# RWKV-7 hybrid layer: other places for the pooling branch in the dense order, and earlier turns for the recurrence

## The chip, the cores and the metric

The kernel runs on one core of a Trainium2 chip. The metric is the device time of one execution in microseconds (us); the time before is the median of 3 runs. TensorE (PE) multiplies matrices, with PEld as its weight loads; VectorE (DVE), ScalarE (ACT) and GpSimd (POOL) work elementwise; SyncE (SP) issues most DMAs. Each engine works off its own queue in order.

## The reference

One step of a hybrid decoder layer for 1024 prompt tokens and 8 x 8 sample tokens, 1088 columns in all, with the same weights. Cut to what matters here:

```
h = rms_norm(x, norm_mix) * (1 + sc) + sh
P = h @ w_in                          # RWKV columns | pooling columns | gate columns
# branch A: RWKV-7, 8 heads of 64
for t:                                # wkv7_scan
    sa = S @ (-kk_t)
    S = S * w_t + sa x (kk_t * a_t) + v_t x k_t
    y_t = S @ r_t
o_r = (group_norm(y) * ln_w + ln_b + bonus) * g
# branch B: pooling over 2, 4, 8 and 16 tokens, four groups of 128 channels
pooled = (cs[t] - cs[t - win]) / count - pp
o_p = einsum("btgc,gcd->btgd", pooled, pool_w) * pool_scale
# merge, then the mixer
merged = sigmoid(gate_A) * (o_r @ w_br_rwkv) + sigmoid(gate_B) * (o_p @ w_br_pool)
x = x + gt * (merged @ w_out)
x = x + gt2 * (relu(h2 @ w_ff1)**2 @ w_ff2);  y = rms_norm(x)
```

## The kernel before

Features lie on the 128 partitions, tokens along the columns. A dense product is done in three parts, high weights by high and low activations and low weights by high activations (whi and wlo against hx), over three chunks of columns (364, 362, 362) into three PSUM tiles called mm. A block of 128 columns of weights is a job: its weights are loaded, split (whi by ScalarE L227, wlo by VectorE L228) and multiplied, and each chunk is then copied out by its own consumer (L573 for projections, L606 and L684 for others).

Phase 1, to about 720 us, holds the input projection and all of the recurrence. Its dense jobs are a list: X are the RWKV columns, Q(g) the columns of pooling group g, G the gates, and at the end op_load (which loads the pooled rows) and eight branch jobs op_job, whose consumer is L1405. Beside the jobs stand four foreground programs written as coroutines, which issue small work in between: the chain of the recurrence over 16 chunks of 64 tokens; the pools, which run, per group, three pooling matmuls of 364, 362 and 298 + 64 columns (px by plw), each copied out by ScalarE (L683) and VectorE (L684); the heads, which for each of four head pairs f go through front (group norms and decay: products wt by sw into two banks, tanh by ScalarE L725), burst (the scan of the decay on VectorE, L751 to L767), unit (products of two sets of 8 chunks), inverse, level and affine; and or_rows.

Affine has two rounds u, each first(u) (64x64 products into two banks, copied by ScalarE L1005 to L1007) and second(u): 16 products ab by at into two banks, four chunks to a bank, read by VectorE L1025 and L1026. Beside affine stand front(f + 1) and the group norm, joined by a helper called both.

The small work has four PSUM banks under two tags, w (2) and wc (2); the mm tiles have four. When a bank is freed decides whether the next step can start. A class Pace makes the order of TensorE's work when the program is built: it counts a virtual time t with estimated lengths, and lets the foreground go on when its step's time has come and a bank is free by its own estimate (free()); otherwise it fills in dense work. A step yields the time after which it goes on, and that time is also taken as the time at which its bank is free again (between 1500 and 3600 ns). The order on the other engines, and which bank a tile gets, are made by the framework's scheduler from there.

Of the kernel before, what the change touches and what calls it, by code (L numbers as in the profile page):

```python
# [83 lines left out]
class Pace:  # L84
# [3 lines left out]
    def __init__(self):  # L88
        self.t = 0.0
        self.work = []  # L90
        self.dense = False
        self.taken, self.banks, self.gap, self.held = None, {"w": [0.0, 0.0], "wc": [0.0, 0.0]}, 1500, False

    def take(self):

# [6 lines left out]

    def free(self):
        return min(self.banks[x][0] for x in (["w"] if self.held else ["w", "wc"])) <= self.t

    def give(self, r):
        for tag in self.taken:
# [24 lines left out]
    def run(self, back, fore=(), until=lambda: False):  # L132
        self.back = back
        live = {i: 0.0 for i in range(len(fore))}
        busy = True
        while (live or busy) and not until():
            for i in sorted(live):
                r = live[i]
                if self.taken is not None and i and not self.free() and (i == 2 and not isinstance(r, Off) and not hasattr(r, "own") or i == 1 and not callable(r) and self.t < r + 1200):
                    continue  # L140
                if r() if callable(r) else r <= self.t:
                    if self.taken is not None:
                        self.taken, self.gap = [], 1500
                    try:
                        r = next(fore[i])
                        if self.taken:
                            self.give(min(max(self.gap if callable(r) else r, 1500), 3600))
                        live[i] = r if callable(r) else type(r)(self.t + r)
                    except StopIteration:
                        del live[i]  # L150
                    break
            else:
                r = "idle"
                if busy:
                    try:
                        r = next(back)
                    except StopIteration:
                        busy = False
                self.dense = r != "idle"
                if r == "idle" and live:  # L160
                    self.t += 100
# [9 lines left out]
class K:  # L171
# [526 lines left out]
    def front(self, f, got=None):  # L698
# [18 lines left out]
        for i, (c0, n) in enumerate(((0, 512), (512, 512), (1024, 64))):  # L717
# [3 lines left out]
            yield 800  # L721
        for c0, n in FP:
            ps = self.ps("w")
# [95 lines left out]
    def unit(self, f, d, u):  # L819
# [13 lines left out]
        Q = dict(ab=tl("ab", [2, 128]), ak=tl("ak", [64], 1), uv=tl("uv", [2, 64]), ra=d["qs"][u]["ra"])  # L833
# [8 lines left out]
        for a in range(0, C, 4):  # L842
            m = min(4, C - a)
            us = slice(a, a + m)
            cu = slice(c0 + a, c0 + a + m)
            pss = [self.ps("w") for _ in HB]
            for i in range(m):
                for hs, ps in zip(HB, pss):
                    self.mm(ps[:, i * 128:(i + 1) * 128], bk[hs, c0 + a + i, :, :].rearrange("p s j -> p (s j)"),
                            ra[hs, a + i, :, :].rearrange("p s j -> p (s j)"), start=True, stop=True)  # L850
            for h, (hs, ps) in enumerate(zip(HB, pss)):
                os = HB[1 - h]
                pv = ps[:, :m * 128].rearrange("p (c s j) -> p c s j", s=2, j=64)
                pr, pa = (pv[:, :, h, :], pv[:, :, 1 - h, :]) if not prompt else (pv[:, :, 0, :], pv[:, :, 1, :])
                nc.vector.tensor_tensor(ab[:, us, h, 0:64], pr, incl.unsqueeze(1).to_broadcast([P, m, 64]), op=ALU.mult)
                nc.vector.tensor_tensor(ak[hs, us, :], pa[hs], strict[hs].unsqueeze(1).to_broadcast([64, m, 64]), op=ALU.mult)
                for b in range(2):
                    rq = slice(os.start + 32 * b, os.start + 32 * b + 32)
                    src = pa[rq, :, 32 * b:32 * b + 32]
                    if prompt:  # L860
                        nc.scalar.activation(ad[rq, cu, :], src, AF.Copy)
                        if b == 0:
                            nc.scalar.activation(ao[rq, cu, :], pa[rq, :, 32:64], AF.Copy)
                    else:
                        nc.vector.tensor_tensor(ad[rq, 16, :], src[:, 0, :], strict[rq, 32 * b:32 * b + 32], op=ALU.mult)
            yield 3500
        bh = bk[:, cs, :, :].rearrange("p c s j -> p c (s j)")
        if prompt:
            nc.vector.tensor_tensor(bh, bh, end[:, cs].unsqueeze(2).to_broadcast([P, C, 128]), op=ALU.mult)
# [122 lines left out]
    def affine(self, f, d):  # L992


        nc, z = self.nc, d["z"]

        def first(u):
            Q = d["qs"][u]
            uv, w = Q["uv"], Q["at"]
            pw, pu = self.ps("w"), self.ps("w")  # L1000
            for i in range(8):
                for h, os in enumerate((HB[1], HB[0])):
                    self.mm(pw[os, i * 64:(i + 1) * 64], z[os, 8 * u + i, :], w[os, i, :], start=True, stop=True)
                    self.mm(pu[os, i * 64:(i + 1) * 64], z[os, 8 * u + i, :], uv[os, i, h, :], start=True, stop=True)
            nc.scalar.activation(w, cut(pw), AF.Copy)  # L1005
            nc.scalar.activation(uv[HB[1], :, 0, :], cut(pu[HB[1], :]), AF.Copy)
            nc.scalar.activation(uv[HB[0], :, 1, :], cut(pu[HB[0], :]), AF.Copy)  # L1007

        def second(u):
            Q = d["qs"][u]  # L1010
            ab, ra, w = Q["ab"], Q["ra"], Q["at"]
            dg = cut(self.hv())
            for hs in HB:
                nc.gpsimd.tensor_tensor(dg[hs], self.kc("ident")[hs, hs].unsqueeze(1).to_broadcast([64, 8, 64]),
                                        d["end"][hs, 8 * u:8 * u + 8].unsqueeze(2).to_broadcast([64, 8, 64]), op=ALU.mult)
            pss = [self.ps("w") for _ in range(2)]
            for i in range(8):
                for h, hs in enumerate(HB):
                    os = HB[1 - h]
                    self.mm(pss[i // 4][hs, i % 4 * 128:(i % 4 + 1) * 128], w[os, i, :], ab[os, i, h, :], start=True, stop=True,  # L1020
                            tile_position=(os.start, hs.start))
            for a, ps in enumerate(pss):
                pv = ps.rearrange("p (c s j) -> p c s j", s=2, j=64)
                us = slice(4 * a, 4 * a + 4)
                nc.vector.tensor_tensor(ra[:, us, 1, :], pv[:, :, 1, :], dg[:, us, :], op=ALU.add)  # L1025
                nc.vector.tensor_tensor(ra[:, us, 0, :], ra[:, us, 0, :], pv[:, :, 0, :], op=ALU.add)  # L1026

        for u in range(2):
            first(u)
            yield 2500  # L1030
            second(u)
            self.done.add(("s", f, u))
            yield 3600

    def chain(self, f, d):

# [100 lines left out]
    def post(self, f):  # L1137
# [28 lines left out]
        def norm(c0, n):  # L1166

            for a, m in FP:
                if c0 <= a < c0 + n:
# [82 lines left out]
    def both(self, a, fill):  # L1252

        pace = self.pace
        live = [[a, pace.t], [fill, pace.t]]
        now = lambda: [x for x in live if (x[1]() if callable(x[1]) else x[1] <= pace.t) and (isinstance(x[1], Off) or pace.free())]
        some = lambda: bool(now())
        some.own = True
        while live:
            ready = now()  # L1260
            if not ready:
                yield some
                continue
            x = ready[0]
            try:
                r = next(x[0])
                x[1] = r if callable(r) else type(r)(pace.t + r)
                if pace.taken:
                    pace.gap = 1500 if callable(r) else r
                    yield some  # L1270
            except StopIteration:
                live.remove(x)
# [57 lines left out]
    def phase1(self, ctx):  # L1330
# [10 lines left out]
        X = self.rwkv_cols  # L1341
        J12, J4 = X(12, act=tanh_lo), X(4, tags=("mm", "w", "w"))

        G = [self.gate(18 + i, self.d_th[i]) for i in range(16)]
        Q = [self.pool_cols(g) for g in range(4)]
        jobs = [X(0), X(8), X(5), X(1), X(9), X(6), X(2), X(10), X(13, act=sigm), X(7), X(3), X(11)]
        for g in range(4):
            jobs += [Q[g], G[2 * g], G[2 * g + 1]] if g < 3 else [G[6], Q[3], G[7]]
        jobs += G[8:]
        order = [(j, h, q) for h in range(2) for q in range(4) for j in (J4, J12)] + [(j, h) for j in jobs for h in range(2)]  # L1350
        order += [(self.op_load, 0)] + [(self.op_job(m), 0) for m in range(8)]
        with ExitStack() as cs:
# [689 lines left out]
def cut(t):  # L2042
    return t.rearrange("p (c j) -> p c j", j=64)
# [12 lines left out]
NC = 17  # L2056
FH = [(0, 512), (512, 576)]
FP = [(0, 512), (512, 288), (800, 288)]
LS = (2000, 2000, 2000, 1500)
FW = 5500  # L2060
WB = (2, 2)
# [77 lines left out]
```

## Time and profile before

| | before |
|---|---|
| time, median of 3 | 1620.5 us (1619.76 to 1621.67) |
| profiled execution: its own time | 1620.03 us |
| profiled execution: span | 1618.2 us |
| TensorE busy | 1583.4 us, 98% |
| weight loads (PEld) | 1481.7 us, 92% |
| VectorE / ScalarE / GpSimd busy | 1022.9 / 736.1 / 356.5 us |
| mean granted TensorE clock | 0.996 |

The span is that of the profiled execution, from its first instruction to its last; its own time is a little longer. In rows of a timeline the first number is the start and the second the length in us, then engine, line, operation, out<-in, partitions x elements and count; what stands in brackets is the idle time of the engine before it and what ended it. A wait row has the sum, the number and the longest.

### The profile page before, as it was taken

How to read it: one execution, taken by the hardware profiler on the slowest of the kernel's cores; microseconds unless marked ns; L12 is line 12 of the kernel's file. 1: busy time of each engine (PE TensorE's matmuls, PEld its weight loads, DVE VectorE, ACT ScalarE, POOL GpSimd, SP SyncE). 2: the span in 40 equal slices, each digit the busy share in tenths (PEclk: the TensorE clock that was granted, in tenths of full speed). 3: DMA queues.
4: the chain of work that ended last, by engine and by line, in shares of the span. 5: the costliest groups of instructions: out<-in, count | busy, mean ns of one | idle time of the engine just before them, and what ended most of it. 6: DMA issues, size and time to landing. Idle time of an engine off the chain costs nothing.

```text
span 1618.2 us, 35474 instructions
## 1 busy us (share of the span) xinstructions
PE 1583.4 (98%) x14331; PEld 1481.7 (92%) x14331; DVE 1022.9 (63%) x1747; ACT 736.1 (45%) x1491; POOL 356.5 (22%) x464
## 2 busy tenths in 40 slices
PE   5999999999999999999999999999999999999997
PEld 3999888998898889979989999999999999999997
DVE  5685674846565636244635597777555777787866
ACT  5543343344335433432325475554455765553323
POOL 3301200120001000101513322333233243521231
PEclk9999999999999999999999999999999999999998
DMA  9334423423423242746875466667666865674313
GB/s 336 110 119 145 140 65 107 132 83 115 126 101 115 76 138 89 294 144 216 332 261 175 144 199 215 206 223 256 234 209 234 312 201 186 197 265 154 100 40 111
DMA packets 123333, 279.43 MB, mean 173 GB/s; under 512 B 16769, under 2 KB 31105, under 8 KB 123169
## 3 DMA queue, kind: packets, MB, share of 16 engines
q1 hardware_dynamic: 107808, 228.52, 41.7%
q0 software_dynamic: 9312, 32.41, 6.0%
q10 hardware_dynamic: 6048, 16.23, 2.8%
q8 instruction: 113, 1.85, 0.5%
q14 instruction: 52, 0.42, 0.1%
HBM read 198.15 MB, written 78.95 MB: 171 GB/s over the span
## 4 chain that ended last, share of the span: by engine, by line
PE 61%; DVE 2%; issue 2%; ACT 2%; DMA 1%; POOL 1%; DVEq 0%; SPq 0%; ACTq 0%; POOLq 0%
PE pr L204 30%; PE mm L204 22%; PE w L204 4%; PE wc L204 4%; DVE hx L1815 0%; DMA wr<-in_w_ff 0%; POOL wlo L228 0%; PE wc L211 0%; DVE hx L1984 0%; DMA wraw<-in_w_ff 0%; PE w L211 0%; POOL wr L1788 0%; DMA d_th<-px 0%; ACT hx L1738 0%; ACT mr L1738 0%
## 5 line engine op out<-in xcount | busy, mean ns | idle before, releaser
L204 PE MATMUL mm<-hx,whi 128*128 128x362 f32 (+1 forms) x1920 | 504.8, 344 | 0.8 <-ACT px L573 0.8
L204 PEld LDWEIGHTS mm<-hx,whi 128*128 128x128 f32 x1920 | 330.1, 189 | 34.0 <-issue 16.1
L204 PE MATMUL pr<-mr,whi 128*128 128x272 f32 x1792 | 336.4, 287 | 0.5 <-DVE hx L1815 0.2
L204 PE MATMUL mm<-hx,wlo 128*128 128x362 f32 (+1 forms) x960 | 314.1, 327 | 0.0
L204 PEld LDWEIGHTS pr<-mr,whi 128*128 128x128 f32 x1792 | 280.8, 188 | 2.7 <-issue 2.7
L204 PE MATMUL pr<-mr,wlo 128*128 128x272 f32 x896 | 257.9, 288 | 0.0
L227 ACT ACTIVATE whi<-wraw 128x512 fp32r<-128x512 f32 x186 | 116.8, 629 | 222.1 <-PE mm L204 86.3
L228 DVE TENSOR_TENSOR wlo<-wraw,whi 128x512 fp32r<-128x512 f32 x145 | 107.5, 742 | 132.2 <-ACT whi L227 130.3
L204 PEld LDWEIGHTS mm<-hx,wlo 128*128 128x128 f32 x960 | 181.3, 189 | 0.0
L204 PE MATMUL pr<-hx,whi 128*128 128x272 f32 x896 | 168.8, 287 | 1.4 <-DVE rs L2010 0.8
L204 PEld LDWEIGHTS pr<-mr,wlo 128*128 128x128 f32 x896 | 168.6, 188 | 0.2 <-DVE wlo L228 0.2
L204 PE MATMUL mm<-mr,whi 128*128 128x272 f32 (+4 forms) x736 | 152.3, 301 | 0.0
L204 PEld LDWEIGHTS pr<-hx,whi 128*128 128x128 f32 x896 | 140.3, 188 | 2.7 <-ACT whi L227 1.0
L227 ACT ACTIVATE whi<-wr 128x512 fp32r<-128x512 f32 x138 | 86.3, 627 | 113.8 <-PE pr L204 76.3
L204 PE MATMUL pr<-hx,wlo 128*128 128x272 f32 x448 | 128.9, 288 | 0.0
L204 PEld LDWEIGHTS mm<-mr,whi 128*128 128x128 f32 x736 | 119.2, 188 | 3.0 <-issue 2.5
L204 PE MATMUL mm<-mr,wlo 128*128 128x272 f32 (+4 forms) x368 | 110.1, 299 | 0.0
L228 POOL TENSOR_TENSOR wlo<-wraw,whi 128x512 fp32r<-128x512 f32 x41 | 54.8, 1337 | 217.8 <-ACT whi L227 217.6
L228 DVE TENSOR_TENSOR wlo<-wr,whi 128x512 fp32r<-128x512 f32 x103 | 76.7, 747 | 18.3 <-ACT whi L227 18.2
L204 PE MATMUL pr<-t,whi 128*128 128x272 f32 x448 | 84.6, 287 | 0.0
L204 PEld LDWEIGHTS pr<-hx,wlo 128*128 128x128 f32 x448 | 84.3, 188 | 0.0
L204 PEld LDWEIGHTS pr<-t,whi 128*128 128x128 f32 x448 | 70.2, 188 | 0.8 <-issue 0.8
(466 smaller groups left out, 2711.0 us busy)
## 6 DMA issues: line engine op xcount, KB each, us to landing
wr<-in_w_ff SPq DMA_DIRECT2D x137, 256.0 KB, 3.5
hid<-d_ch POOLq DMA_DIRECT2D x72, 272.0 KB, 3.9
wraw<-in_w_ff SPq DMA_DIRECT2D x71, 256.0 KB, 3.2
wraw<-in_w_in SPq DMA_DIRECT2D x68, 256.0 KB, 3.1
d_ch<-hx SPq DMA_DIRECT2D x52, 272.0 KB, 3.8
hid<-in_w_ada_mlp SPq DMA_DIRECT2D x24, 512.0 KB, 6.5
d_th<-px SPq DMA_DIRECT2D x22, 544.0 KB, 3.1
wt<-d_x SPq DMA_DIRECT2D x20, 544.0 KB, 4.2
```

Source lines behind the costliest of these rows:

```text
L204: return self.nc.tensor.matmul(out, lhsT, rhs, **kw)
L227: nc.scalar.activation(hi, raw, AF.Copy)
L228: (nc.gpsimd if pool else nc.vector).tensor_tensor(lo, raw, hi.bitcast(F32), op=ALU.subtract)
```

## The change

Two things are changed, and a third is in the code but inactive.

1. A step may now yield two times: the one at which it goes on, and, in `pace.est`, the one at which its bank is taken as free. In unit 3500 becomes 2000 with the bank at 3500, after second(u) in affine 3600 becomes 500 with the bank at 3600.
2. The list of dense jobs: Q(0) stands right behind X(13), ahead of X(2), and X(13) two places earlier; G(0) stands ahead of X(7); behind the X jobs come Q(1), G(1), Q(2), four gates, Q(3) and the other gates, in place of triples of a Q and two gates.
3. `soon` and `some.due`: with PAIR = 0 they never hold anything back.

```diff
-            yield 3500
+            self.pace.est = 3500
+            yield 2000
...
             second(u)
             self.done.add(("s", f, u))
-            yield 3600
+            self.pace.est = 3600
+            yield 500
...
                 if pace.taken:
-                    pace.gap = 1500 if callable(r) else r
+                    pace.gap = pace.est or (1500 if callable(r) else r)
+                    pace.est = None
                     yield some
...
-        jobs = [X(0), X(8), X(5), X(1), X(9), X(6), X(2), X(10), X(13, act=sigm), X(7), X(3), X(11)]
-        for g in range(4):
-            jobs += [Q[g], G[2 * g], G[2 * g + 1]] if g < 3 else [G[6], Q[3], G[7]]
-        jobs += G[8:]
+        jobs = [X(0), X(8), X(5), X(1), X(9), X(6), X(13, act=sigm), Q[0], X(2), X(10), G[0], X(7), X(3), X(11)]
+        jobs += [Q[1], G[1], Q[2], G[2], G[3], G[4], G[5], Q[3]] + G[6:]
...
                 if r() if callable(r) else r <= self.t:
+                    if self.taken is not None and not isinstance(r, Off) and self.soon(live, i):
+                        continue
...
+PAIR = 0
```

Lines below L876 move down by 10 to 13: L684 becomes L694, L751 to L767 become L761 to L777, L1025 and L1026 become L1036 and L1037, L1405 becomes L1417.

The first place is the affine step of head pair 0 with front(1). TensorE before, around second(1) of it (w ab<-at are its two halves, wt by sw the decay of front(1)):

```order
L204 MATMUL mm_317_2596<-hx_3_348,whi_296_2429 128x362
L204 MATMUL mm_317_2596<-hx_4_349,whi_296_2429 128x362
L204 MATMUL mm_317_2596<-hx_3_348,wlo_297_2430 128x362
L204 MATMUL w_324_2659<-ab_215_1672,at_218_1675 64x128 x8
L204 MATMUL w_325_2660<-ab_215_1672,at_218_1675 64x128 x8
L204 MATMUL wc_326_2681<-wt_291_2364,sw_247_1932 128x288
L204 MATMUL wc_327_2684<-wt_291_2364,sw_247_1932 128x288
```

TensorE now, from the first pooling chunk of group 0 on (px by plw), with the second(1) halves in the middle:

```order
L214 MATMUL w_312_2555<-px_265_2051,plw_85_756 128x364
L214 MATMUL w_313_2559<-wt_283_2299,sw_235_1856 128x512
L214 MATMUL wc_314_2562<-wt_283_2299,sw_235_1856 128x512
L214 MATMUL wc_315_2568<-px_265_2051,plw_85_756 128x362
L214 MATMUL w_317_2575<-ab_206_1620,at_209_1623 64x128 x8
L214 MATMUL w_318_2576<-ab_206_1620,at_209_1623 64x128 x8
L214 MATMUL wc_319_2597<-px_265_2051,plw_85_756 128x298
L214 MATMUL wc_319_2597<-ds_296_2398,plw_85_756 128x64
L214 MATMUL wc_320_2602<-wt_283_2299,sw_235_1856 128x288
L214 MATMUL wc_321_2605<-wt_283_2299,sw_235_1856 128x288
```

The three pooling chunks have come in between, and of the dense work only one group of three is left among them (left out here).

VectorE at the same place, before (L751 to L767 are the burst of front(1), L1025 and L1026 read the two halves of second(1)):

```order
L751 TENSOR_SCALAR wt_2366<-wt_2366 128x512
L752 SCALAR_TENSOR_TENSOR wt_2366<-kscan,wt_2366 128x512
L761 TENSOR_SCALAR bk_2741<-wt_2367,hp 128x8x64
L762 TENSOR_TENSOR wt_1933<-wt_1933,bk_2741 128x512
L228 TENSOR_TENSOR wlo_2572<-wraw_2569,whi_2571 128x512
L763 SCALAR_TENSOR_TENSOR wt_2367<-wt_2367,wt_2361 128x512
L766 TENSOR_TENSOR bk_2741<-wt_1933,wt_2366 64x8x64 x2
L767 SCALAR_TENSOR_TENSOR bk_2741<-wt_2367,wt_2366 64x8x64 x2
L1025 TENSOR_TENSOR ra_1669<-w_2659,hv_2656 128x4x64
L1026 TENSOR_TENSOR ra_1669<-ra_1669,w_2659 128x4x64
L1025 TENSOR_TENSOR ra_1669<-w_2660,hv_2656 128x4x64
L1026 TENSOR_TENSOR ra_1669<-ra_1669,w_2660 128x4x64
```

VectorE now (L761 to L777 the burst, L1036 and L1037 the halves, L694 the pooling chunks):

```order
L761 TENSOR_SCALAR wt_284_2301<-wt_284_2301 128x512
L762 SCALAR_TENSOR_TENSOR wt_284_2301<-kscan_746,wt_284_2301 128x512
L771 TENSOR_SCALAR bk_335_2693<-wt_285_2302,hp_331 128x8x64
L772 TENSOR_TENSOR wt_236_1857<-wt_236_1857,bk_335_2693 128x512
L773 SCALAR_TENSOR_TENSOR wt_285_2302<-wt_285_2302,wt_282_2296 128x512
L1036 TENSOR_TENSOR ra_205_1617<-w_317_2575,hv_316_2572 128x4x64
L1037 TENSOR_TENSOR ra_205_1617<-ra_205_1617,w_317_2575 128x4x64
L776 TENSOR_TENSOR bk_335_2693<-wt_236_1857,wt_284_2301 64x8x64 x2
L777 SCALAR_TENSOR_TENSOR bk_335_2693<-wt_285_2302,wt_284_2301 64x8x64 x2
L1036 TENSOR_TENSOR ra_205_1617<-w_318_2576,hv_316_2572 128x4x64
L1037 TENSOR_TENSOR ra_205_1617<-ra_205_1617,w_318_2576 128x4x64
L694 SCALAR_TENSOR_TENSOR px_293_2393<-w_312_2555,part_323,d_292_2392 128x364
```

The reader of the second half now has the products L776 and L777 of the burst ahead of it, and the pooling rows stand behind both.

The second place is head pair 2. TensorE before, where pooling group 3 stands at the level step (w<-z,hv) and the group norm's spread (kct by wt, by sw):

```order
L204 MATMUL wc_6036<-px_5623,plw_5251 128x364
L211 MATMUL w_6040<-kct,wt_5571 128x128 x4
L204 MATMUL w_6048<-z,hv_6015 32x32 x32
L204 MATMUL wc_6083<-px_5623,plw_5251 128x362
L211 MATMUL wc_6087<-kct,wt_5571 128x128 x4
L211 MATMUL w_6093<-kct,sw_5566 128x128
```

TensorE now, with the chunks of group 3 in its affine step, from the first chunk to the last (dense rows between them):

```order
L214 MATMUL w_6043<-px_5547,plw_4990 128x364
L214 MATMUL mm_5842<-hx_354,whi_5806 128x362
L214 MATMUL mm_5842<-hx_355,whi_5806 128x362
L214 MATMUL mm_5842<-hx_354,wlo_5807 128x362
L214 MATMUL wc_6056<-px_5547,plw_4990 128x362
L214 MATMUL w_6063<-ab_4796,at_4799 64x128 x8
L214 MATMUL wc_6064<-ab_4796,at_4799 64x128 x8
L214 MATMUL w_6085<-px_5547,plw_4990 128x298
L214 MATMUL w_6085<-ds_5833,plw_4990 128x64
```

The chunks have gone from the level step, and stand around second(0).

The third place is VectorE at the first branch jobs. Before, where the branch jobs' consumer (L1405) has the weight split (L228) behind it:

```order
L1405 SCALAR_TENSOR_TENSOR px_8013<-px_8013,mm_8015 128x364
L1405 SCALAR_TENSOR_TENSOR px_8013<-px_8013,mm_8016 128x362
L1405 SCALAR_TENSOR_TENSOR px_8013<-px_8013,mm_8017 128x362
L228 TENSOR_TENSOR wlo_8179<-wraw_8176,whi_8178 128x512
L1100 TENSOR_TENSOR hv_8238<-w_8237,kct 128x512
L1101 TENSOR_REDUCE xr_8206<-hv_8238 128x64
L1102 TENSOR_TENSOR x_8205<-xr_8206,x_8207 64x64
```

And now, where the consumer (L1417) has the group norm's rows (L1185) and the weight split (L238) ahead of it:

```order
L1185 SCALAR_TENSOR_TENSOR wt_7205<-w_8341,wt_7205 128x288
L1185 SCALAR_TENSOR_TENSOR wt_7205<-w_8357,wt_7205 128x288
L238 TENSOR_TENSOR wlo_8370<-wraw_8367,whi_8369 128x512
L1417 SCALAR_TENSOR_TENSOR px_8316<-px_8316,mm_8318 128x364
L1417 SCALAR_TENSOR_TENSOR px_8316<-px_8316,mm_8319 128x362
L1417 SCALAR_TENSOR_TENSOR px_8316<-px_8316,mm_8320 128x362
L1417 SCALAR_TENSOR_TENSOR px_8377<-px_8377,mm_8379 128x364
```

The row on which the bank of the first job's first chunk hangs has moved behind the group norm's.

More of the change, by code (lines that the diff above doesn't have):

```diff
@@ L92, in __init__ @@
         self.taken, self.banks, self.gap, self.held = None, {"w": [0.0, 0.0], "wc": [0.0, 0.0]}, 1500, False
+        self.est = None
     def take(self):
@@ L104, in free, with soon @@
         return min(self.banks[x][0] for x in (["w"] if self.held else ["w", "wc"])) <= self.t
+    def soon(self, live, i):
+        if not self.dense or i == 1:
+            return False
+        ts = [getattr(r, "due", lambda: None)() if callable(r) else None if isinstance(r, Off) else r for j, r in live.items() if j != i and j < 3]
+        return any(t is not None and self.t < t <= self.t + PAIR for t in ts)
     def give(self, r):
@@ L1258, in both @@
         some.own = True
+        some.due = lambda: min([x[1] for x in live if not callable(x[1]) and not isinstance(x[1], Off)], default=None)
         while live:
```

## The prediction

> **What bounds the kernel now.** I read the page's head first, then the table of 40 us stretches over phase 1, then TensorE's waits, then the timeline at the two longest of them.
>
> ```profile
> span 1618.2 us, 35474 instructions
> PE 1583.4 (98%) x14331; PEld 1481.7 (92%) x14331; DVE 1022.9 (63%) x1747; ACT 736.1 (45%) x1491; POOL 356.5 (22%) x464
> ```
>
> The reader sees that TensorE is busy in 98% of the span so nothing else can bound it. A change of order that leaves TensorE's instructions as they were can therefore only win or lose in TensorE's idle time, and in the time for which its clock is lowered. Phase 1, where all that moves lies, ends at about 720 us. Of its fourteen stretches from 160 to 720 us, the worst and the sum (columns: stretch, its length, then busy time and instructions of TensorE, of its weight loads, of VectorE, ScalarE and GpSimd, the granted clock, the DMA share, GB/s):
>
> ```profile
> 480.00:520.00 40.00, 37.67 (x626) 34.37 (x626) 24.72 (x37) 21.27 (x39) 8.34 (x11) 0.96 0.23 68
> sum 560.00, PE 554.93 PEld 488.14 DVE 321.04 ACT 234.29 POOL 46.52; mean PE 39.64 PEld 34.87 DVE 22.93 ACT 16.74 POOL 3.32
> ```
>
> TensorE is busy for 554.93 of 560 us: 5.1 us are all that could be gained there from idle time, the clock apart. The worst stretch has 37.67 of 40 us and a mean granted clock of 0.96. The list of what TensorE waits for names the smaller ones:
>
> ```profile
> PE wc L204 <- DVE wt L1184: 1.1, 1, 1.1
> PE mm L204 <- ACT px L573: 0.8, 1, 0.8
> PE wc L204 <- ACT wt L333: 0.5, 1, 0.5
> PE wc L204 <- ACT wt L725: 0.4, 1, 0.4
> PE wc L204 <- DVE px L684: 0.3, 1, 0.3
> ```
>
> And the timeline of TensorE, then that of VectorE, at the worst place, the recurrence of head pair 2:
>
> ```profile
> 504.95 0.78 PE L204 MATMUL wc<-px,plw 128*128 128x364 f32 x2
> 505.56 0.60 PE L211 MATMUL w<-kct,wt 128*128 128x128 f32 x4
> 507.11 1.20 PE L204 MATMUL w<-z,hv 32*32 32x32 f32 x64 [0.95 <-ACT hv L979]
> 508.24 0.88 PE L204 MATMUL wc<-px,plw 128*128 128x362 f32 x2
> 510.50 1.01 PE L211 MATMUL wc<-kct,wt 128*128 128x128 f32 x4 [1.39 <-DVE px L684]
> ```
> ```profile
> 509.85 0.60 DVE L684 SCALAR_TENSOR_TENSOR px<-wc,part,d 128x364 fp32r<-128x364 f32 x1 [0.75 <-ACT d L683]
> ```
>
> A pooling matmul, a spread of the group norm, the level step of the recurrence and another pooling matmul stand there without dense work between them. The spread at 510.50 needs the bank of the pooling matmul of 504.95, and VectorE's L684 frees it only when ScalarE's L683 is done, which came late. TensorE loses 0.95 + 1.39 = 2.34 us. Then the clock falls:
>
> ```profile
> 504.00:512.00 8.00, 5.67 (x86) 4.53 (x85) 3.93 (x8) 6.83 (x12) 1.31 (x2) 0.92 0.21 68
> 512.00:520.00 8.00, 8.00 (x103) 7.41 (x103) 4.56 (x7) 4.99 (x8) 0.00 (x0) 0.87 0.52 156
> ```
>
> 8 us at 0.92 and 8 us at 0.87 make 8 x 0.08 + 8 x 0.13 = 1.68 us. This place costs 2.34 + 1.68 = 4.0 us.
>
> **The change, part by part.** TensorE has 8111 rows in the order before and after, VectorE 1710, ScalarE 1477, GpSimd 446, SyncE 700, and TensorE goes over from dense work to small work as often as before. So there is no term for more or fewer instructions, and what lies after phase 1 costs nothing, its order being the same. The inactive code (PAIR is 0) costs nothing. The DMAs that go with the moved steps (pooling weights, the stores and loads of rows on SyncE's queue) cost nothing in TensorE's time except at the end of phase 1, taken up below: none of the waits listed above is for a DMA. All that counts is which waits go and which come.
>
> *Goes: head pair 2's place.* The pooling chunks of group 3 stand away from the level step now; the first of them has nine dense matmuls behind it. The 4.0 us go. What comes in their stead, in the affine step of the same pair: the first(1) matmuls take the bank of a pooling chunk that stands just ahead of them, and wait for L694 (the old L684), and the spread behind waits for ScalarE. By the row at 509.85 an L684 lasts 0.60, and the ScalarE copy that it needs 0.56 (below), together 1.16 at best, of which some 0.3 lies beside the second half of the affine step: 0.9 for the first wait. For the spread I take the 0.5 of the row on L333, a wait of the same form. Net: -4.0 + 1.4 = -2.6, from -4.0 (nothing comes) to 0 (the clock falls again).
>
> *Comes: head pair 0's affine step.* Pool group 0 is now ready early, and its three chunks fall into the second half of affine and front(1) (shown under the change). The rows of before for the VectorE and ScalarE work that stands there:
>
> ```profile
> 214.55 0.43 DVE L751 TENSOR_SCALAR wt<-wt 128x512 f32<-128x512 f32 x1 [2.14 <-ACT wt L725]
> 215.01 1.22 DVE L752 TENSOR_TENSOR_SCAN wt<-kscan,wt 128x512 f32<-128x512 bf16 x1
> 216.16 0.52 DVE L761 TENSOR_SCALAR bk<-wt,hp 128x512 f32<-128x512 f32 x1
> 216.71 0.69 DVE L762 TENSOR_TENSOR wt<-wt,bk 128x512 f32<-128x512 f32 x1
> ...
> 217.93 0.68 DVE L763 SCALAR_TENSOR_TENSOR wt<-wt,wt 128x512 f32<-128x512 f32 x1
> ...
> 219.74 1.38 DVE L766 TENSOR_TENSOR bk<-wt,wt 64x512 f32<-64x512 f32 x2
> 221.13 1.39 DVE L767 SCALAR_TENSOR_TENSOR bk<-wt,wt 64x512 f32<-64x512 f32 x2
> ...
> 223.95 0.42 DVE L1025 TENSOR_TENSOR ra<-w,hv 128x256 f32<-128x256 f32 x1
> 224.28 0.41 DVE L1026 TENSOR_TENSOR ra<-ra,w 128x256 f32<-128x256 f32 x1
> ```
> ```profile
> 220.28 1.96 PE L204 MATMUL w<-ab,at 64*64 64x128 f32 x32
> ```
> ```profile
> 213.83 0.69 ACT L725 ACTIVATE wt<-wc,hp 128x512 f32<-128x512 f32 x1 [0.58 <-PE wc L204]
> ...
> 217.49 0.60 ACT L1005 ACTIVATE at<-w 128x512 f32<-128x512 f32 x1
> ```
> ```profile
> 509.25 0.56 ACT L683 ACTIVATE d<-wc,part 128x364 fp32r<-128x364 f32 x1
> ```
>
> VectorE is shown here running such a row about 0.08 us before the last one has ended, so five rows of burst (0.43 + 1.22 + 0.52 + 0.69 + 0.68) take 3.2, the pair L1025 and L1026 0.75, and the four products L766 and L767 2.6. In the changed order the two halves of second(1) are in the same bank, since the first pooling chunk holds the other until its L694, and VectorE does the five rows of the burst before it reads the first half. From the end of first(1): ScalarE copies three tiles (3 x 0.6) and the pooling chunk (0.56), then the tanh (0.69), so at some 3.2 us the burst begins and at 6.4 it is through its five rows, and at 7.2 the first half is read. TensorE in that time does two dense groups (0.5 each), two pooling chunks (0.6 start to start, by 504.95 and 505.56), two decay products (about 0.6 each) and the first half (1.96 / 2), with some 0.2 for the changes between kinds: done by 4.6. It waits 2.6. Then come the second half (1.0) and a chunk (0.6), to 8.8, while VectorE does the four products (9.8), the second half's two rows (10.55) and two L694 (11.65): TensorE's next product waits for that bank, 2.8. Behind each of these waits TensorE's queue holds all that follows, the decay products of front(1) and then the dense stream, so each is lost in full. Together 5.4 us; before, the same step waited for 0.4. Bounds: 2.6, if the tanh ends early enough for the first half to be read on time, and 5.7, if the burst begins as late as the first half. I take 5.4.
>
> *The clock there.* The trace of before has it fall after idle times of 0.95 and 1.39 within 5 us, at a cost of 1.68; here 2.6 and 2.8 fall within 8 us. By that row a fall is due, 1.7; I take 1.0, between nothing and that. The Trainium skill, page "TensorE: Matmul & The Clock Gate", section "Part 1: The HAM clock gate", says that the clock goes to half after an idle window of about 3.4 us. By that rule neither place would lower the clock, and the sum would be 1.0 lower; the row at 504 to 512 us shows a fall without such a gap, so the row stands.
>
> *Comes: pool group 2 in the unit of head pair 2.* The second bank of the unit's products is that of a pooling chunk just issued, with almost nothing between: 0.56 + 0.60 = 1.2, and 0.6 for the two later chunks, which have some matmuls beside them. 1.8, from 0 to 3 (a weight row of 0.69 stands ahead of L694 on VectorE).
>
> *Comes: the end of phase 1.* All loads of the pooled rows now go in one cluster, and the second chunk of branch job 1 needs the bank that the consumer L1417 of job 0 frees. On VectorE that row stands now behind the group norm's L1185 and the weight row that follows it; before, it stood ahead.
>
> ```profile
> 691.00 0.53 DVE L1405 SCALAR_TENSOR_TENSOR px<-px,mm 128x362 f32<-128x362 f32 x1 [0.54 <-PE mm L204]
> 691.50 0.69 DVE L228 TENSOR_TENSOR wlo<-wraw,whi 128x512 fp32r<-128x512 f32 x1
> ...
> 708.13 0.69 DVE L1173 SCALAR_TENSOR_TENSOR wt<-w,wt 128x512 f32<-128x512 f32 x1 [1.47 <-PE w L204]
> ```
> ```profile
> 706.01 0.63 ACT L227 ACTIVATE whi<-wraw 128x512 fp32r<-128x512 f32 x1 [0.90 <-PE mm L204]
> ...
> 709.00 0.62 ACT L1174 ACTIVATE wt<-wt 128x512 f32<-128x512 f32 x1
> ```
>
> The chain is L1185 (0.45 for its 288 columns), a square (0.45), the weight copy (0.63), the weight row (0.69) and the consumer (0.53): 2.75, beside eleven dense matmuls of 0.165, 1.8. So 0.95, and some 0.5 for ScalarE, whose load of a gate row stands ahead of the last gate's copies: 1.5, from 0 to 3.
>
> *The rest.* The two waits on L333 and L725 have other work beside them now: -0.9. The two of head pair 1 (1.1 and 0.3) stay as one of 1.4. A copy of a projection (the 0.8 of L573) stands again behind ScalarE's work, at another place: +0.8.
>
> Sum: -2.6 + 5.4 + 1.0 + 1.8 + 1.5 - 0.9 + 0.8 = +7.0 us. The profiled execution took 1620.03 us (span 1618.2), half a microsecond under the median of 1620.5, so 1620.03 + 7.0 = 1627.0.
>
> **The rivals.**
> - *Nothing moves on balance.* The tanh comes early, only 2.6 is left at head pair 0, no clock falls, and the end of phase 1 and the unit cost nothing: -2.6 + 2.6 - 0.9 + 0.8 = -0.1, so 1620. For it: TensorE's work is the same to the row. Against it: the order of VectorE puts the burst ahead of the bank's reader, whatever the times are.
> - *Faster.* The place of head pair 2 is healed outright (-4.0, -0.9) and VectorE has the burst behind it before TensorE comes to second(1), as it would if TensorE came there more than 6 us later against VectorE than I count: 1620.03 - 4.9 + 0.8 = 1616. For it: those 4.0 us are the largest single loss of phase 1. Against it: the burst cannot start before front(1), which TensorE itself issues three rows earlier.
> - *Worse.* The clock falls at head pair 0 and again at the end of phase 1 (1.7 each), the waits come at their upper bounds (5.7, 3, 3), and head pair 2 gains nothing: 0 + 5.7 + 3.4 + 3 + 3 - 0.1 = 15, so 1635.
>
> **How the numbers follow.** A measurement of this kernel tells about 0.2% from no change, 3.2 us. Forecast (up to 7.0, give or take 3): 0.62. Nothing on balance: 0.14. Faster: 0.12. Worse: 0.12. The forecast's own spread reaches from 1623 to 1632; to leave out no more than 2 in 10 the range goes to 1618 below and to 1633 above. Faster by over 0.2% (below 1617.3): 0.12. Within it (1617.3 to 1623.7): nothing on balance and a little of the forecast, 0.16. Slower: 0.72.
>
> **What would show it.** Right: in the profile after, TensorE has two waits of 2 to 3 us on L1037 and L694, just after the first pooling matmul, and the 0.95 and 1.39 at head pair 2 are gone with the fall of the clock there. Wrong at the largest term: no wait above 1 us at second(1). Wrong at the clock: 1.00 in all stretches around it. Wrong at the end of phase 1: no wait on L1417. If the time is 1616 or less, VectorE was ahead at head pair 0, or the falls of the clock that I did not see elsewhere have gone.

## The result, and the profile after

The changed kernel takes 1636.74 us (median of 4 runs, 1635.06 to 1639.17), against 1621.09 for the kernel before beside it on the same chip: 1.0097 times, 95% interval 1.0084 to 1.0110. It is slower by about 16 us. The prediction had slower, but 1627.0, and 1636.7 lies above its range. The profiled execution took 1635.06 us (span 1633.3), 15.0 us more than that of before.

From the list of TensorE's waits (sum in us, times, the longest), the five on VectorE rows of phase 1 behind its start:

```profile
PE w L214 <- DVE ra L1037: 2.8, 1, 2.8
PE wc L214 <- DVE px L694: 2.6, 2, 1.7
PE w L214 <- DVE px L694: 2.3, 3, 1.2
PE wc L214 <- DVE px L664: 2.3, 1, 2.3
PE mm L214 <- DVE px L1417: 2.3, 2, 1.2
```

They make 12.3 us; before, such entries made 2.8 (1.4, 1.1 and 0.3). The wait at the start, 13.7 us now and 13.5 before, is left out. The stretches (columns as in the prediction) say where:

```profile
200.00:240.00 40.00, 35.53 (x333) 27.32 (x332) 24.15 (x40) 15.74 (x36) 1.68 (x5) 0.87 0.21 68
480.00:520.00 40.00, 36.55 (x663) 33.86 (x663) 24.24 (x38) 19.08 (x34) 9.00 (x11) 0.96 0.25 82
```

From 200 to 240 us TensorE is busy for 35.53 of 40 us and its clock is 0.87; and the stretch of head pair 2, the worst of before with 37.67 and 0.96, is no better. First head pair 0, TensorE and then VectorE:

```profile
207.52 0.78 PE L214 MATMUL w<-px,plw 128*128 128x364 f32 x2
...
210.59 1.09 PE L214 MATMUL w<-ab,at 64*64 64x128 f32 x16
214.43 1.09 PE L214 MATMUL w<-ab,at 64*64 64x128 f32 x16 [2.75 <-DVE ra L1037]
215.45 1.36 PE L214 MATMUL wc<-px,plw 128*128 128x298 f32 x2
...
218.81 1.82 PE L214 MATMUL wc<-wt,sw 64*128 64x288 f32 x4 [1.67 <-DVE px L694]
...
229.38 0.33 PE L214 MATMUL wc<-S,ra 64*64 64x64 f32 x4
```
```profile
210.17 0.43 DVE L761 TENSOR_SCALAR wt<-wt 128x512 f32<-128x512 f32 x1 [5.32 <-ACT wt L735]
...
213.54 0.42 DVE L1036 TENSOR_TENSOR ra<-w,hv 128x256 f32<-128x256 f32 x1
...
214.20 1.38 DVE L776 TENSOR_TENSOR bk<-wt,wt 64x512 f32<-64x512 f32 x2
...
216.99 0.43 DVE L1036 TENSOR_TENSOR ra<-w,hv 128x256 f32<-128x256 f32 x1
...
218.17 1.09 DVE L694 SCALAR_TENSOR_TENSOR px<-wc,part,d 128x362 fp32r<-128x362 f32 x2
```

The reader sees the queue that the prediction described, row by row: the burst from 210.17, the first half of second(1) read at 213.54, and TensorE's second half starting at 214.43, when that is done; then the products, the second half, the pooling rows, and TensorE's next product at 218.81. The waits are 2.75 and 1.67 us. What was not foreseen stands in the lengths: the chunk at 215.45 takes 1.36 us, where the same chunk takes 0.77 in run 1 below. The clock was at half:

```profile
216.00:224.00 8.00, 6.33 (x19) 5.10 (x18) 3.23 (x7) 1.56 (x3) 0.80 (x3) 0.50 0.38 150
```

Taken in pieces of 2 us, the clock stands at half for 10.2 us, from about 215.4 to 225.7; before, it had one fall of 3.4 us in phase 1. Then head pair 2, TensorE, VectorE and GpSimd:

```profile
503.32 0.66 PE L221 MATMUL wc<-kct,wt 128*128 128x128 f32 x4
...
508.29 0.34 PE L214 MATMUL wc<-at,z 64*64 64x64 f32 x4 [2.27 <-DVE px L664]
...
518.98 0.34 PE L214 MATMUL wc<-at,z 64*64 64x64 f32 x4 [0.89 <-DVE px L694]
```
```profile
496.65 1.23 DVE L653 TENSOR_TENSOR d<-px 128x1038 f32<-128x1038 f32 x1
...
498.16 2.07 DVE L653 TENSOR_TENSOR px<-d 128x1036 f32<-128x1036 f32 x1
...
507.40 0.74 DVE L1196 SCALAR_TENSOR_TENSOR wt<-wt,part,wc 128x512 f32<-128x512 f32 x1
```
```profile
498.00 6.24 POOL L1025 TENSOR_TENSOR hv<-kct,end 64x512 f32<-64x512 f32 x4
```

The products of first(0) at 508.29 need the bank of the spread of 503.32, whose reader L1196 runs at 507.40, behind the pooling sums of group 3 (the profile names L664, the short row behind it on VectorE, which ends at 508.23). Two of these sums take 2.07 us (L653, at 498.16, and the next as long) instead of 1.23 at 496.65, for as long as GpSimd works on the decay's diagonal beside them. TensorE waits 2.27 us there, the clock falls again (0.81 over 504 to 512 us), and waits of 0.89 and 0.41 us follow.

### The profile page after: what moved, and what is told of

It is laid out like the page before. It is cut to its first block, busy times and chain, and to the rows that moved or that the text cites. A ratio compares the mean times of both kernels' runs of the same rounds, so it can differ in the third digit from the quotient of the medians.

```text
span 1633.3 us, 35469 instructions
## 1 busy us (share of the span) xinstructions
PE 1590.8 (97%) x14331; PEld 1485.8 (91%) x14331; DVE 1025.7 (63%) x1747; ACT 736.4 (45%) x1491; POOL 356.4 (22%) x464
## 4 chain that ended last, share of the span: by engine, by line
PE 50%; DVE 2%; ACT 1%; issue 1%; DMA 1%; POOL 0%; DVEq 0%; ACTq 0%; POOLq 0%
PE pr L214 33%; PE mm L214 14%; PE w L214 2%; PE wc L214 1%; DMA d_th<-px 1%; DVE hx L1827 0%; DVE hx L1996 0%; POOL wr L1800 0%; ACT hx L1750 0%; ACT mr L1750 0%; ACT whi L237 0%; DMA wr<-in_w_ff 0%; DMA d_u<-hid 0%; DVE hx L1751 0%; PE wc L221 0%
## 5 line engine op out<-in xcount | busy, mean ns | idle before, releaser
L238 DVE TENSOR_TENSOR wlo<-wraw,whi 128x512 fp32r<-128x512 f32 x145 | 109.4, 755 | 124.1 <-ACT whi L237 121.9
L238 POOL TENSOR_TENSOR wlo<-wraw,whi 128x512 fp32r<-128x512 f32 x41 | 55.6, 1355 | 237.4 <-ACT whi L237 237.2
L238 DVE TENSOR_TENSOR wlo<-wr,whi 128x512 fp32r<-128x512 f32 x103 | 76.4, 745 | 16.8 <-ACT whi L237 16.7
```

The source lines that it names most:

```text
L238: (nc.gpsimd if pool else nc.vector).tensor_tensor(lo, raw, hi.bitcast(F32), op=ALU.subtract)
```

## The experiments

Each run stood beside runs of the kernel before on the same chip. The ratios are to those.

**1. The banks of group 0 freed by ScalarE alone.** For group 0 the low part is made from the copy in SBUF, so the low part of that group is not the reference's.

```diff
-  nc.vector.scalar_tensor_tensor(lo[:, c0:c0 + n], ps[:, :n], sc, hi..., op0=ALU.mult, op1=ALU.subtract)
+  x = hi[:, c0:c0 + n].bitcast(F32) if g == 0 else ps[:, :n]
+  nc.vector.scalar_tensor_tensor(lo[:, c0:c0 + n], x, sc, hi..., op0=ALU.mult, op1=ALU.subtract)
```

> The changed kernel, but for pool group 0 the low part is computed from the copy in SBUF (hi times scale less hi, so the low part of that group is not the reference's), not from the PSUM bank. ScalarE's copy alone then frees the banks of its three chunks; VectorE has the same rows in the same order. Theory 1 (VectorE's late reading of the pooling chunks holds the banks, the idle time there is 2.75 + 1.67 us, and the fall of the clock, 5.1 us, follows from it): no wait above 0.5 us at second(1) and front(1) of head pair 0, granted clock 1.00 from 200 to 240 us, time 9 to 9.5 us under the changed kernel, about 1627. Rival 1 (the clock falls for the many small products there, whatever the waits): only the 4.4 us of waits go, about 1632. Rival 2 (VectorE's order itself makes TensorE wait, not the bank): no change, about 1636.5.

Measured: 1629.24 us, 1.0041 (1.0024 to 1.0057). TensorE at the same place:

```profile
208.72 0.77 PE L214 MATMUL w<-px,plw 128*128 128x364 f32 x2
...
211.79 1.96 PE L214 MATMUL w<-ab,at 64*64 64x128 f32 x32
213.69 0.77 PE L214 MATMUL wc<-px,plw 128*128 128x298 f32 x2
...
222.54 0.33 PE L214 MATMUL wc<-S,ra 64*64 64x64 f32 x4
```

Both halves run through in one piece (32 records, 1.96 us), no wait is left, and the clock is 1.00 in all pieces from 200 to 240 us. From the first pooling chunk to the same product of the chain it is 222.54 - 208.72 = 13.82 us, against 229.38 - 207.52 = 21.86 in the changed kernel: 8.04 us, of which 4.42 are waits and so 3.6 the clock. Theory 1 holds, with a total of 8.0 where 9 to 9.5 was expected: TensorE waited for 1.67 of the 10.2 us at half clock and was busy for 8.6, half of which is 4.3; why it is only 3.6 isn't shown. The clock of this run is no matter of one execution: the mean granted clock of its eight executions is 0.994 to 0.997, that of the changed kernel's four 0.991 to 0.993.

**2. Zero products in place of the waits.**

```diff
+  if f == 0 and u == 1 and i == 4:      # second(1), between its halves
+      self.fillin(14)                    # 14 products with zero weights into an open dense sum
...
+  if f == 1 and c0 == 512:               # front(1), third chunk
+      self.fillin(9)
```

> The changed kernel with 14 products with zero weights (128x362, added to an open dense sum) between the two halves of second(1) of head pair 0 and 9 ahead of the third decay chunk of front(1), which are the two places where TensorE waited 2.75 and 1.67 us; the order of all else is the same. Theory 1 (the idle time makes the clock fall): the zero products take the place of the waits, 23 x 0.15 = 3.5 us of 4.4, the clock stays at 1.00 there and the time falls by the 5.1 us of the clock, to about 1631.5. Rival 1 (it falls for the small products): clock still 0.5 for some 10 us, time 1636.5 or up to 3.5 us more. By the rule of the Trainium skill, page TensorE: Matmul & The Clock Gate, section Part 1: The HAM clock gate, an idle window of 3.4 us is needed for a fall; without idle time there is none, as in theory 1.

Measured: 1638.04 us, 1.0104 (1.0079 to 1.0129): not below the changed kernel, where 1631.5 was expected. But at the place itself the expectation holds:

```profile
208.00:216.00 8.00, 7.77 (x61) 5.76 (x60) 5.99 (x10) 4.01 (x7) 0.00 (x0) 1.00 0.01 2
216.00:224.00 8.00, 7.07 (x93) 5.90 (x91) 3.67 (x8) 2.42 (x5) 0.80 (x3) 1.00 0.38 149
```

The clock stays at 1.00, waits of 0.23 and 0.93 us are left, and the stretch from the first pooling chunk to the chain takes 19.04 us: 2.8 less than in the changed kernel, and 13.82 + 1.16 of waits + 23 x 0.15 = 18.4 of the 19.04 are accounted for. So the small products alone don't make the clock fall there (in run 8 they stand there too, at 1.00), and without the idle time it stays up. The 2.8 us don't show in the whole time: the intervals overlap. In the profiled execution 2.0 of them are still there behind phase 1 (the changed kernel's first row of L1507 starts at 829.06 us, the same row here at 827.09); then a wait of 2.2 us on VectorE at 922 us and another fall of the clock take them away. The mean granted clocks of the six executions go from 0.990 to 0.997; where it fell in those that have no profile isn't known.

**3. GpSimd's diagonal of head pair 2 cut short.** Head pair 2's state is left without its decay.

```diff
+  if f == 2:
+      nc.gpsimd.memset(dg, 0.0)
-  for hs in HB:
+  for hs in HB if f != 2 else ():
       nc.gpsimd.tensor_tensor(dg[hs], ...)
```

> The changed kernel, but for head pair 2 GpSimd fills the diagonal of the decay with zeros in one memset in place of two products of 64x512 per round (so head pair 2's state is left without its decay). VectorE's order is the same. Theory 2 (at head pair 2 the four GpSimd products, 6.2 us at 498 us, slow VectorE's pooling sums beside them from 1.2 to 2.1 us each, so that the spread's bank comes free late): the rows L653 there take 1.2 to 1.3 us, the wait of 2.27 us before first(0) falls to about 0.3, the clock does not fall, and the time is 2 + 1.7 us lower, about 1633. Rival (the sums of group 3 simply stand ahead of the spread's reader, at any speed): the wait stays above 1.5 us, the clock falls, time within 1 us of 1636.5.

Measured: 1632.95 us, 1.0068 (1.0049 to 1.0088), VectorE and GpSimd at the place:

```profile
499.18 1.23 DVE L653 TENSOR_TENSOR px<-d 128x1036 f32<-128x1036 f32 x1
...
500.70 1.22 DVE L653 TENSOR_TENSOR d<-px 128x1032 f32<-128x1032 f32 x1
```
```profile
499.00 0.52 POOL L1025 MEMSET hv<- 128x512 f32 x1
```

The sums take 1.23 and 1.22 us again, the wait before first(0) is gone, the clock is 1.00 from 496 to 528 us. Theory 2 holds. (At head pair 0 this execution has its two waits as before, 2.74 and 1.97 us, but the clock is at half for 6.8 us in place of 10.2.) The Trainium skill, page "GPSIMD Engine Reference", section "1. Specifications", names GpSimd's interfaces to SBUF as shared with VectorE, with contention for VectorE instructions of two SBUF inputs; L653 has two, and 1.23 against 2.07 us agrees.

**4. The new list, with the earlier turn in unit alone.**

```diff
-            self.pace.est = 3600
-            yield 500
+            yield 3600
```

> The changed kernel with its new list of jobs and the earlier turn in unit, but with the old turn after second(u) in affine (3600). Theory 1 (the pooling chunk and front(1) fall between first(1) and second(1) of head pair 0, because of the turn of 500): head pair 0 waits below 0.7 us in all, clock 1.00 there; time about 1625 (1622 to 1628). Rival 3 (the new list of jobs alone puts pool group 0 there and makes the loss): second(1) still waits over 2 us with a fall of the clock, time above 1633.

Measured: 1626.54 us, 1.0036 (1.0020 to 1.0052), as theory 1 has it. Head pair 0 keeps one wait:

```profile
212.15 0.75 PE L214 MATMUL wc<-wt,sw 64*128 64x288 f32 x2 [0.47 <-ACT uv L1018]
```

The clock is 1.00 there; head pair 2 still has its wait of 2.27 us. The early turn after second(u), with the new list, is thus what costs 10 us. The 6 us left over before are not divided between the new list and the turn in unit.

**5. The old list with both earlier turns.**

```diff
-        jobs = [X(0), X(8), X(5), X(1), X(9), X(6), X(13, act=sigm), Q[0], X(2), ...]
-        jobs += [Q[1], G[1], Q[2], G[2], G[3], G[4], G[5], Q[3]] + G[6:]
+        the two statements of before
```

> The changed kernel with the list of jobs of before: only the two earlier turns are left of the change. Theory 1 (the loss comes where a step of the recurrence needs a bank whose reader stands behind pooling work on VectorE, and where that falls is decided by turns and list together): head pair 0 has no pooling group ready, so no wait over 0.7 us at its second(1); but in its order the pooling sums (L653 to L664) of groups 1 and 3 now stand ahead of readers at head pairs 1 and 2, as those of group 3 do in the changed kernel, so there are waits of several us on L664 there, and the time is 10 to 25 us over before. Rival 4 (the earlier turns are harmless, the new list makes the loss): within 3 us of before.

Measured: 1656.39 us, 1.0226 (1.0210 to 1.0242): 35 us over before, more than the 10 to 25 expected. Rival 4 falls: given the turns, the new list is a gain of 20 us. Head pair 0 has no wait at second(1), as expected. The waits are at head pairs 1 and 2, but of another kind than expected, on TensorE and VectorE ("issue": the profile names no releaser):

```profile
391.64 1.55 PE L214 MATMUL w<-px,plw 128*128 128x364 f32 x2 [7.51 <-issue]
```
```profile
376.16 1.24 DVE L653 TENSOR_TENSOR d<-px 128x1038 f32<-128x1038 f32 x1
...
391.37 0.17 DVE L664 COPY px<-zf 128x3 f32<-128x3 f32 x1
```

Not a bank's reader is late but the pooled rows themselves: the sums of group 1 begin at 376.16, rows of the burst and the sample's rows stand between them, the last copy (L664) is at 391.37, and the pooling matmul starts at 391.64 after 7.5 us (at group 3, 10.3). Run 6, which has the same list and the same turn in affine, but the old one in unit, has no such wait: the turn in unit brought the pooling matmul ahead of what VectorE could have ready. What that turn does by itself, with the old turn in affine, was not run.

**6. The old list with the earlier turn in affine alone.** The `yield 500` with its 3600 is put into the kernel before, nothing else.

> The kernel before with the earlier turn after second(u) in affine alone (500 in place of 3600, the bank still taken at 3600). Theory 1: no pooling chunk stands between the halves of second(1) at head pair 0, so no wait above 0.7 us there; at head pair 2 the place of before (0.95 + 1.39 us and a fall of the clock) is gone and waits below 1 us come; time from 4 us under before to the same, 1617 to 1621. Rival 5 (the turn of 500 itself brings the burst ahead of second(1)'s reader on VectorE): over 2 us of waits at head pair 0, time 4 us or more over before.

Measured: 1621.43 us, 1.0008 (0.9998 to 1.0018): no difference. Rival 5 falls: with the old list the turn does no harm. Its waits are 1.24 and 0.74 us on pooling chunks and 0.95 + 0.70 at head pair 2, with 1.01 on ScalarE's L634 between them, and one fall of the clock stays, so the 4 us are not gained.

**7. The kernel before with group 3 later.**

```diff
-            yield (8500, 9800, 9800, 10800)[g]
+            yield (8500, 9800, 9800, 12500)[g]
```

> The kernel before with one number changed: pooling group 3 waits 12500 in place of 10800 before its matmuls, so that they leave the level step of head pair 2. If the reading of before is right (0.95 + 1.39 us of waits and 1.7 us of clock there), those 4 us go, 1617; if the wait only moves on to the next step, the same as before, 1621.

Measured: 1617.65 us, 0.9982 (0.9971 to 0.9993). The stretch of head pair 2, 37.67 at 0.96 before:

```profile
480.00:520.00 40.00, 39.22 (x651) 35.57 (x651) 25.90 (x39) 20.05 (x37) 8.34 (x11) 1.00 0.19 64
```

Two waits of 0.4 us are left there of 2.34, and no fall. 2.9 us are gained (1.1 to 4.7): the reading of the kernel before was right, and this version beats both kernels, the one before by 0.2%.

**8. The changed kernel with the chunks out of PSUM early.** It computes what the reference does.

```diff
-  nc.scalar.activation(hi[:, c0:c0 + n], ps[:, :n], AF.Copy, scale=sc)
-  nc.vector.scalar_tensor_tensor(lo[:, c0:c0 + n], ps[:, :n], sc, hi..., op0=ALU.mult, op1=ALU.subtract)
+  nc.scalar.activation(lo[:, c0:c0 + n].bitcast(F32), ps[:, :n], AF.Copy, scale=sc)
+  nc.vector.tensor_copy(hi[:, c0:c0 + n], lo...)
+  nc.vector.tensor_tensor(lo[:, c0:c0 + n], lo..., hi..., op=ALU.subtract)
```

> The changed kernel, with the whole result computed as in the reference, but the pooling chunks leave PSUM by one ScalarE copy of full precision, from which VectorE makes the high and the low part in SBUF (two rows per chunk in place of one). Theory 1: the banks come free without VectorE, for all four groups, so at head pair 0 the two halves of second(1) wait less: most of 8 us goes there, 1 us at head pair 2 and 1 at its unit; VectorE has 12 rows of some 0.4 us more; time 1626 to 1630. Rival: the rows more on VectorE make other readers late by as much, 1634 or above.

Measured: 1632.25 us, 1.0072 (1.0058 to 1.0087), between the two. Head pair 0:

```profile
217.24 1.09 PE L214 MATMUL w<-ab,at 64*64 64x128 f32 x16 [2.75 <-DVE ra L1038]
...
220.20 1.20 PE L214 MATMUL wc<-wt,sw 64*128 64x288 f32 x4 [1.00 <-ACT px L693]
```
```profile
208.00:216.00 8.00, 6.49 (x90) 4.40 (x86) 2.96 (x5) 4.31 (x7) 0.00 (x0) 1.00 0.01 2
216.00:224.00 8.00, 5.76 (x52) 4.59 (x54) 6.62 (x15) 2.97 (x6) 0.56 (x1) 1.00 0.21 77
```

The first wait, which I expected to go, is as long as ever: the second half is still released by the reading of the first (L1038). The second shrank from 1.67 to 1.00. ScalarE's rows, in the changed kernel and then in this run, show why:

```profile
208.63 0.55 ACT L693 ACTIVATE d<-w,part 128x364 fp32r<-128x364 f32 x1
```
```profile
219.13 0.56 ACT L693 ACTIVATE px<-w,part 128x364 f32<-128x364 f32 x1 [3.14 <-PE wc L214]
```

In the changed kernel ScalarE copies the first pooling chunk soon after its matmul of 207.52. Here that matmul is at 210.33 and the copy comes only at 219.13, after an idle time that, by the profile, TensorE's third chunk ends (its last 64 columns run at 218.87). So the first chunk's bank is not freed early at this place, whatever the edit was meant to do, and the first wait could not go this way; why the copy waits for the third chunk was not looked into. With 3.75 us of waits within 6 us the clock is 1.00. In run 1 the wait of head pair 2 is 2.27 us, as in the changed kernel, also without a fall. So the same wait can bring a fall of the clock or none.

**9 and 10. The same on kernels 6 and 7.** The edit is that of run 8.

> The kernel before with the affine turn of 500 (as in old_jobs_affine_turn) and with the pooling chunks leaving PSUM by ScalarE alone, high and low part made in SBUF. If the waits of 1.24 and 0.7 us that stayed in old_jobs_affine_turn come from VectorE holding pooling banks, they fall by 1 to 2 us and the time to 1619 or 1620; if the rows more on VectorE make up for it, no change, 1621.5.

> The kernel of old_jobs_later_group3 with the pooling chunks leaving PSUM by ScalarE alone. It had one wait on a pooling chunk left, 0.35 us, and 1.08 us on the spread's reader: so at most 0.4 us to gain, 1617 to 1618; if the 12 rows more on VectorE delay readers of the recurrence, 1619 or more.

Measured: 1620.68 us, 1.0003 (0.9993 to 1.0012), and 1618.24 us, 0.9984 (0.9974 to 0.9995). In 9 the wait of 1.24 is 0.61 and that of 0.70 is 0.26, as expected, but no time can be told from it; 10 is as 7. Nothing is gained by it beyond version 7.

The new list with both old turns was not run either, so the list alone has no number.

## Why the prediction was wrong, point by point

| term of the sum | predicted, us | measured, us | shown by |
|---|---|---|---|
| head pair 0, waits, less 0.4 of before | +5.0 | +4.0 | run 1, rows above |
| head pair 0, the clock | +1.0 | +3.6 | runs 1 and 2 |
| head pair 2 | -2.6 | +1.3 | run 3 for its cause |
| pool group 2 in unit | +1.8 | +1.4 | profile |
| the end of phase 1 | +1.5 | +2.3 | profile |
| L333 (L725 is in the first row) | -0.5 | -0.5 | profile |
| head pair 1; copy of a projection; a wait on L1081 | +0.8 | +0.4 | profile |
| rows longer without a listed wait | 0 | about 2.5 | not settled |
| sum | +7.0 | +15.0 | |

- **The mechanism at head pair 0 was right.** The first wait was 2.75 (2.6 predicted), the second 1.67 (2.8). The burst took 3.37 us to the first half's reading (3.2 predicted; of the rows shown for it only some overlap by 0.08). The second wait is shorter because TensorE's second half and the chunk behind it took 2.7 us (214.43 to 217.14, from 215.43 on at half clock) and not 1.6.
- **The step that failed by most, 3.9 us, is "The 4.0 us go" at head pair 2, net -2.6.** They went, as pooling group 3 left the level step, and the two waits named in their stead came as predicted: 0.89 at first(1) (0.9) and 0.41 at the spread (0.5). But the group's sums stand ahead of an earlier spread's reader now, and slowed by GpSimd: another wait of 2.27 and again 1.7 of clock, 5.3 in all in place of 1.4. I followed the chunks' matmuls and not the sums that come before them on VectorE.
- **The step that failed next, by 2.6 us, is the term of the clock at head pair 0.** "I take 1.0, between nothing and that", with 1.7 as the upper end, took one fall of 3.4 us. There were 10.2 us, and they cost 3.6: the waits followed each other, and while the clock was low the next one came. By the rule of the Trainium skill, page "TensorE: Matmul & The Clock Gate", section "Part 1: The HAM clock gate", there would have been no fall, and run 8 has 3.75 us of waits without one; but the changed kernel has one with waits of 2.75 and 1.67, so a whole idle window isn't needed. That the window runs free, which the same section of the Trainium skill states, agrees with a wait of 2.27 us that made a fall at 508 us in the changed kernel and none at 501 us in run 1.
- **What decides between a fall and none** can be worked out from the traces. Within a profile the falls start whole multiples of 3.413 us apart: in the changed kernel at 215.43 and 508.98 us, 86 of them; in run 8 at 79.37 and 506.04, 125 of them. Laid on that grid, the changed kernel's first wait leaves 2.41 us idle in one piece of 3.413 us (212.02 to 215.43), and its wait of 2.27 us at head pair 2 lies in one piece too; a fall follows each. The same wait of 2.75 us in run 8 is cut by the grid into 1.42 and 1.33, that of 2.27 us in run 1 into 0.90 and 1.37; no fall follows. In the twelve traces, from 25 to 1600 us, the piece behind every one with 1.73 us or more of idle time is at half clock; behind those with 1.4 to 1.7 us some are and some aren't. Where the grid lies could not be known ahead, so whether such a wait brings a fall is luck. Not explained is the last third of the 10.2 us: no idle time stands in the piece before it, and run 3's execution, with nearly the same waits, hasn't got it.
- **The end of phase 1** has the two waits on L1417 as described, 1.23 and 1.03.
- **The copy of a projection**, +0.8, didn't come a second time: the wait on L573 of before, 0.82 at 77.8 us, is that on L583 now, 0.77 at 78.1 us. The 0.4 measured in that row are small waits on other rows.
- **The rest isn't settled.** TensorE is busy for 7.4 us more (1590.8 against 1583.4), of which 3.6 are the clock and 1.3 stand in the first 80 us, where as much less was waited for. About 2.5 us lie in rows of small products that are longer without a wait being listed. Run 4, with no fall of the clock at head pair 0, has such rows too: from 80 us to the first row of L1495 (813.5 us before, 820.67 in run 4) TensorE is busy for 731.84 us, 3.5 more than before.
- **The "worse" rival's 1635** was near by its sum and not by its reasons: of its two falls of the clock the one at the end of phase 1 didn't come, and its 0 for head pair 2 was 1.3.
- **Which edit it is:** neither alone. The early turn in affine costs nothing with the old list (run 6) and 10 us with the new (run 4 against the change); the new list gains 20 us when both turns are early (run 5 against the change). With the old list and the early turn in affine, the turn in unit costs 35 us (run 5 against run 6).

## What to carry to other kernels

When a step is moved ahead in an order, follow all its work in each engine's queue, not just the instructions named in the wait: here the sums that feed a pooling matmul held up another step's bank on VectorE. Where two waits of a few microseconds stand close together on TensorE, count a lowered clock for longer than the waits themselves (here 10.2 us, which cost 3.6), and keep the range open, since the same wait may bring a fall or none. And the loss that the profile shows at one place may go by moving one number there (run 7: 3 us), where a rearrangement of the whole order moved it elsewhere and added to it.

## What the runs showed of the hardware

- VectorE's sums of two SBUF inputs took 1.23 us alone (run 3) and 2.07 beside GpSimd's 64x512 products (the changed kernel).
- The clock fell for multiples of 3.4 us: 3.4 (before), 6.8 (run 3, head pair 0), 10.2 (the changed kernel, head pair 0), and the falls of a profile start whole multiples of 3.413 us apart. With 23 zero products in the idle time it stayed up (run 2).
- The same idle time of 2.27 us, before the same products, made the clock fall in one kernel (all of it in one piece of the 3.413 us grid) and not in another (0.90 and 1.37 in two); 3.75 us in two waits within 6 us, with at most 1.46 in a piece, made none in run 8.
